# A hybrid Fourier and state-space layer on one core: the product of C with the entering states changes sides

## The chip, the core and the metric

The kernel runs on one core of one Trainium2 chip. The metric is the device time of one execution in microseconds (us), the median over the runs shown. The profiled execution is a further one, and its time stands beside its span below.

## The reference, cut to what matters

One layer works on 1152 tokens (128 of context, 1024 of latents) with 1024 features. After a normalisation and one wide product, one branch takes a Fourier transform, the other a bidirectional state-space scan (SSD) in chunks of 128 tokens; both are gated, merged and projected. The part that the change touches is the last line but one of the scan: the states that enter a chunk are read by that chunk's C, and each token and head is scaled by exp(acs), the decay since the chunk's start (in either direction).

```
acs = cumsum(dt * a) within the chunk
y_diag = einsum("bclgn,bcsgn,bgrcls,bcsgrp->bclgrp", cc, bc, lmat, xdt)
y_off  = einsum("bclgn,bcgrpn,bgrcl->bclgrp", cc, states_in, exp(acs))
y = y_diag + y_off
```

There are 8 groups (g) of 4 heads with 64 features each, states of 128, 9 chunks (c), and two directions (d). Chunk 0 is the context, for which no entering state is read.

## The kernel before, in words

**Engines and names.** PE is TensorE, DVE VectorE, ACT ScalarE, POOL GpSimd, SP the engine whose queue issues nearly all loads and stores. All data is float32. Large products run as three matmuls in the type float32r on split operands (high and low part, helper mm3, lines 99 to 103; the split itself is a ScalarE cast and a VectorE subtraction, lines 87 to 90); small products run as plain float32 matmuls, which the trace shows as two instructions each. The order of TensorE's instructions is the program's; the order on the other engines is laid out when the program is built, by when their inputs are expected (line 66 takes TensorE alone out of that).

**The SSD stage.** For each group g (lines 643 to 680) TensorE computes the columns of the wide product for B (tile bt), two chunks of x (xs), C (ct), some gate columns and z, each as a GEMM of 3 tiles x 8 x 3 matmuls of 384 columns. The small work of the scan is sewn into these GEMMs by a clock: `tick()` advances after every six such matmuls, and `at(step, t1, t2, ...)` resumes a Python generator at those ticks. So a GEMM has 12 ticks, and three ticks are 18 large matmuls plus what is sewn in between.

**The steps.** `tr_b` and `tr_x` (lines 514 to 534) transpose B and x to token-major (bn, xb). `states` (542 to 566) builds the entering states st[k] of both directions one after the other: weighted x (xw), split (xhl, in the e buffers), products (PSUM tile st), and a VectorE multiplication by decB and an addition. `outputs` (568 to 609) runs once per group and chunk, in the order 0, 4, 5, 3, 6, 2, 7, 1, 8, one chunk every three ticks, each in three sub-steps three ticks apart:
- first: load ab (acs of the chunk, broadcast to all partitions, 512 KB, two buffers) and, for c > 0, ea (exp(acs), two loads of 128 KB, three buffers); GpSimd masks ab into e (two selects, lines 582 and 583; three e buffers), eight ScalarE exponentials, one VectorE addition e+e;
- second: the product of B and C (cb, line 590), and VectorE multiplies it into e;
- third: for c > 0 the product po of the entering states with C, the states being the stationary side (line 597): four float32 matmuls with the result in the layout features by tokens; VectorE multiplies it by ea (599), GpSimd adds the two directions (600); four float32 matmuls y of x with e (605); VectorE adds y, then ea, to xs (607, 609).

Sub-steps of neighbouring chunks share a tick: third of one, second of the next, first of the one after.

**Around it.** dt_phase (348 to 435) computes the decays once, feature-major, and stores acs to d_acs and exp(acs) to d_eac, from where ab and ea are loaded; dt_natural (437 to 446) transposes two of its results to token-major (kwN). After a group's outputs, `gated` multiplies by z, `norm` normalises (616 to 641), and the next group's second GEMM writes xs again. All small products draw their PSUM tiles from five shared buffers (gps, line 121). After the last group four gate GEMMs cover the loads of the Fourier branch (685 on), which reuses the memory.

Of the kernel before, what the change touches and what calls it, by code (L numbers as in the profile page):

```python
# [12 lines left out]
F32 = mybir.dt.float32  # L13
F32R = mybir.dt.float32r
# [48 lines left out]
def tile_step(ctx, tc, a, o):  # L63
# [61 lines left out]
    d_acs = dp.tile([NCH, 64, P], F32, name="d_acs")  # L125
    d_eac = dp.tile([NCH, 64, P], F32, name="d_eac")
    d_dec = dp.tile([64, 8], F32, name="d_dec")
# [11 lines left out]
    make_identity(nc, ident)  # L139
    ones = cp.tile([P, P], F32, name="ones")  # L140
    V.memset(ones, 1.0)
    onesr = cp.tile([P, P], F32R, name="onesr")
    V.tensor_copy(onesr, ones)
    eps1 = cp.tile([P, 1], F32, name="eps1")
# [90 lines left out]
    sc = cp.tile([P, KT, 32], F32, name="sc")  # L235
    with pool("sp") as sp:
        xt = []
        for k in range(KT):
# [108 lines left out]

    def dt_phase(buf, w, kwN, decB):
        dtc = cp.tile([P, 3], F32, name="dtc")
# [3 lines left out]
        act(dtc[:, 2:3], dtc[:, 1:2], AF.Exp)  # L353
        xall, eall = buf[:, 0 : 5 * P], buf[:, 5 * P : 10 * P]
        G.memset(xall[64:P, 4 * P :], 0.0)
# [19 lines left out]
        def part(k0, k1):  # L375
# [27 lines left out]
            for h0 in (0, 64):  # L403
# [6 lines left out]
                V.tensor_copy(tot[bw, k0:k1].unsqueeze(2), sv[bw, :, 0:1])  # L410
            act(y_, s_, AF.Exp)
            for h0, c0, c1 in ((0, k0, k1), (64, 5 + k0, min(5 + k1, NCH))):
                for dst, src in ((d_acs, s_), (d_eac, y_)):
                    nc.sync.dma_start(dst[c0:c1].rearrange("c q l -> q c l"),
                                      src.rearrange("p (c l) -> p c l", l=P)[h0 : h0 + 64, 0 : c1 - c0])
            tt(x_, x_, s_, ALU.subtract)
# [17 lines left out]
        at(part(2, 5), DTT[1])  # L434
        at(dt_natural(xall, eall, kwN), DTT[2])

    def dt_natural(xall, eall, kwN):
        for k0, k1 in ((0, 2), (2, 5)):
            for w, src in enumerate((xall, eall)):
                ps = gps(f"dtt{k0}{w}")  # L440
                for k in range(k0, k1):
                    PE.transpose(ps[:, (k - k0) * P : (k - k0 + 1) * P], src[:, k * P : (k + 1) * P], ident)
                pv = ps[:, 0 : (k1 - k0) * P].rearrange("p (c h q) -> p h c q", h=2, q=64)
                for h, c0, c1 in ((0, k0, k1), (1, 5 + k0, min(5 + k1, NCH))):
                    V.tensor_copy(kwN[:, c0:c1, w * 64 : w * 64 + 64], pv[:, h, 0 : c1 - c0])
        yield
# [28 lines left out]
    with pool("sd") as sd, pool("ss") as ss, pool("sx", side="right") as sx:  # L475
# [3 lines left out]
        kwv = kwN.rearrange("p c (w d g h) -> p c w d g h", w=2, d=2, g=NG)  # L479
        knv, wsv = kwv[:, :, 0], kwv[:, :, 1]  # L480

        cr = [ss.tile([P, PADW + 1], F32, name=f"cr{i}") for i in range(2)]
        for t_ in cr:
# [3 lines left out]
        dt_phase(ss.tile([P, NCH, 256], F32, tag="xb", name="dtx").rearrange("p c q -> p (c q)"),  # L487
                 ss.tile([P, 8, P], F32R, tag="ct", name="w_dt"), kwN, decB)
        gate(3)
# [52 lines left out]
        def states(g, k, xb, bn, sts):  # L542

            cf, cb = (0, 0) if k < 0 else (1 + k, 8 - k)
            xw = ss.tile([P, 2, 256], F32, tag="xw", name=f"xw{g}_{k}", bufs=1)
            xhl = ss.tile([P, 2, 2, 256], F32R, tag="e", name=f"xhl{g}_{k}", bufs=3)
            xh, xl = xhl[:, 0], xhl[:, 1]
            for d, c in ((0, cf), (1, cb)):
                tt(xw[:, d].rearrange("p (j h q) -> p j h q", j=2, h=2), xb[:, c].rearrange("p (j h q) -> p j h q", j=2, h=2),
                   wsv[:, c, d, g, :].rearrange("p (h j) -> p j h", h=2).unsqueeze(3).broadcast_to([P, 2, 2, 64]), ALU.mult)  # L550
            split(xh, xl, xw)
            yield
            ps = gps(f"st{g}_{k}")
            if k < 0:
                mm3(ps, (bn[:, 0, 0], bn[:, 1, 0]), [x.rearrange("p d q -> p (d q)") for x in (xh, xl)], True, True)
                so = ss.tile([P, 1024], F32, tag="ab", name=f"so{g}", bufs=2)[:, 0:512]
                S.copy(so, ps)
                nc.sync.dma_start(o["sout"][g], so)
                return
            st = sts[0]  # L560
            for d, c in ((0, cf), (1, cb)):
                mm3(ps[:, d * 256 : d * 256 + 256], (bn[:, 0, c], bn[:, 1, c]), (xh[:, d], xl[:, d]), True, True)
            tt(st[:, k + 1].rearrange("p d (h q) -> p d h q", h=4), st[:, k].rearrange("p d (h q) -> p d h q", h=4),
               decv[:, :, g, :, k].unsqueeze(3).broadcast_to([P, 2, 4, 64]), ALU.mult)
            sv = st[:, k + 1].rearrange("p d q -> p (d q)")
            tt(sv, sv, ps, ALU.add)

        def outputs(g, c, bt, ct, xs, xb, st):
# [4 lines left out]
                              d_acs[c].rearrange("(d g q) l -> g d (q l)", d=2, g=NG)[g].partition_broadcast(P))  # L573
            if c > 0:

                ea = ss.tile([P, 2, 2, P], F32, tag="ea", name=f"ea{g}_{c}", bufs=3)
                for r0 in range(2):
                    nc.sync.dma_start(ea[r0 * 64 : r0 * 64 + 64].rearrange("p d j l -> p d (j l)"),
                                      d_eac[c].rearrange("(d g h j) l -> g h d (j l)", d=2, g=NG, h=2)[g, r0].partition_broadcast(64))
            e = ss.tile([P, 2, 4, P], F32, tag="e", name=f"e{g}_{c}", bufs=3)  # L580
# [9 lines left out]
            PE.matmul(pcb[:, 0:P], bt[:, cc], ct[:, cc], start=True, stop=True)  # L590
            tt(e[:, 0], e[:, 0], pcb[:, 0:P].unsqueeze(1).broadcast_to([P, 4, P]), ALU.mult)
            yield
            if c > 0:
                po = gps(f"po{g}_{c}")
                for d, k in ((0, c - 1), (1, 8 - c)):
                    for j in range(2):
                        PE.matmul(po[:, (2 * d + j) * P : (2 * d + j + 1) * P], st[:, k, d, j * P : j * P + P],  # L597
                                  ct[:, cc], start=True, stop=True)
                tt(ea, po.rearrange("p (d j l) -> p d j l", d=2, j=2), ea, ALU.mult)
                G.tensor_tensor(ea[:, 0], ea[:, 0], ea[:, 1], op=ALU.add)  # L600
            py = gps(f"y{g}_{c}")
            for j in range(2):
                for h in (2 * j, 2 * j + 1):
                    r0 = (h % 2) * 64
                    PE.matmul(py[r0 : r0 + 64, j * P : j * P + P], xb[:, c, h * 64 : h * 64 + 64], e[:, 0, h % 2 * 2 + j],  # L605
                              start=True, stop=True, tile_position=(0, r0))
            tt(xs[:, :, cc], xs[:, :, cc], py[:, 0 : 2 * P].rearrange("p (j l) -> p j l", j=2), ALU.add)
            if c > 0:
                tt(xs[:, :, cc], xs[:, :, cc], ea[:, 0], ALU.add)

# [32 lines left out]
        for g in range(NG):  # L643
# [21 lines left out]
            for i, c in enumerate((0, 4, 5, 3, 6, 2, 7, 1, 8)):  # L665
                t = 20 + 3 * i
                at(outputs(g, c, bt, ct, xs, xb, st), t - 6, t - 3, t)
            done = clock[0] + t
            gate(GATES[g])
# [479 lines left out]
```

## Time and profile before

| what | value |
|---|---|
| median of 3 runs | 1737.99 us (1735.97 to 1738.11) |
| profiled execution, its own time | 1733.38 us |
| its span, first to last instruction | 1731.6 us |
| granted TensorE clock over the span | 0.996 of full speed |
| SSD stage, groups 0 to 7 | about 115 to 1102 us of the span |

The profile covers one execution. "Busy" is the time in which an engine has an instruction under way; TensorE's are pipelined and overlap, so their durations add up to more than the time they take, and start-to-start distances are the better measure. "PEld" is the loading of stationary operands. A line such as "A <-B 4.4, 5" under the waits means that A stood idle until B was done, 4.4 us in 5 waits.

### The profile page before, as it was taken

The numbers are of one execution on the slowest core, as the hardware profiler recorded it, in microseconds if no ns is written. First come the engines' busy times: TensorE is split into PE (matmuls) and PEld (weight loads), VectorE is DVE, ScalarE is ACT, GpSimd is POOL, SyncE is SP. The second block draws the span as 40 slices with busy tenths as digits, with TensorE's granted clock in tenths as the row PEclk, the third lists the DMA queues.
The fourth block names the chain that finished last, engine by engine and source line by source line (L and its number), as shares of the span: only waits on it lengthen the run. The fifth ranks groups of instructions, "written<-read, shape, count | busy, mean of one in ns | idle before, by whom it ended". The sixth has DMA issues, their size and how long they took to land.

```text
span 1731.6 us, 27916 instructions
## 1 busy us (share of the span) xinstructions
PE 1706.1 (99%) x10728; PEld 1641.4 (95%) x10728; DVE 1093.1 (63%) x1876; ACT 809.8 (47%) x1666; POOL 184.7 (11%) x266
## 2 busy tenths in 40 slices
PE   7999999999999999999999999999999999999998
PEld 5999999999999999999999999999988999999987
DVE  6665877866857757757757758687487324444432
ACT  5445665565566576566466565415333211112221
POOL 1200210300300300301301202402000000000000
PEclk9999999999999999999999999999999999999999
DMA  9242633523524624524523525461066646643432
GB/s 349 80 102 59 152 103 104 142 92 99 149 76 114 140 70 118 141 77 114 135 75 106 140 77 146 148 228 54 16 214 217 229 146 229 220 168 120 161 122 73
DMA packets 110136, 229.63 MB, mean 133 GB/s; under 512 B 20594, under 2 KB 56436, under 8 KB 108340
## 3 DMA queue, kind: packets, MB, share of 16 engines
q1 hardware_dynamic: 108708, 223.14, 42.7%
q0 software_dynamic: 1296, 4.72, 0.7%
q8 instruction: 84, 1.38, 0.3%
q14 instruction: 48, 0.39, 0.1%
HBM read 187.24 MB, written 40.58 MB: 132 GB/s over the span
## 4 chain that ended last, share of the span: by engine, by line
PE 93%; DMA 3%; DVE 2%; issue 1%; ACT 0%; POOL 0%; SPq 0%; DVEq 0%; POOLq 0%; ACTq 0%
PE mm_g L101 5%; PE mm_g L103 5%; PE mm_g L102 5%; PE mm_x L101 4%; PE mm_x L103 4%; PE mm_x L102 4%; PE mm_z L101 3%; PE mm_z L103 3%; PE mm_z L102 3%; PE po L597 2%; PE y L605 2%; PE mm_b L101 2%; PE mm_c L101 2%; PE mm_b L103 2%; PE mm_c L103 2%; PE mm_b L102 2%
## 5 line engine op out<-in xcount | busy, mean ns | idle before, releaser
L73 ACT ACTIVATE e<-e,kwN 128x128 f32<-128x128 f32 x576 | 179.3, 390 | 110.9 <-POOL e L582 108.6
L101 PE MATMUL mm_g<-hT,wh_g 128*128 128x384 f32 x528 | 182.1, 345 | 0.0
L103 PE MATMUL mm_g<-hT,wl_g 128*128 128x384 f32 x528 | 177.9, 337 | 0.0
L102 PE MATMUL mm_g<-hT,wh_g 128*128 128x384 f32 x528 | 177.5, 336 | 0.0
L582 POOL TENSOR_SCALAR_AFFINE_SELECT e<-ab 128x512 f32<-128x512 f32 x72 | 51.0, 709 | 790.0 <-PE st L103 659.2
L101 PE MATMUL mm_z<-hT,wh_z 128*128 128x384 f32 x384 | 133.9, 349 | 0.0
L101 PE MATMUL mm_x<-hT,wh_x 128*128 128x384 f32 x384 | 131.5, 342 | 0.0
L103 PE MATMUL mm_z<-hT,wl_z 128*128 128x384 f32 x384 | 129.4, 337 | 0.0
L103 PE MATMUL mm_x<-hT,wl_x 128*128 128x384 f32 x384 | 129.2, 337 | 0.0
L102 PE MATMUL mm_x<-hT,wh_x 128*128 128x384 f32 x384 | 129.0, 336 | 0.0
L102 PE MATMUL mm_z<-hT,wh_z 128*128 128x384 f32 x384 | 129.0, 336 | 0.0
L101 PEld LDWEIGHTS mm_g<-hT,wh_g 128*128 128x128 f32 x528 | 99.3, 188 | 0.5 <-issue 0.2
L102 PEld LDWEIGHTS mm_g<-hT,wh_g 128*128 128x128 f32 x528 | 99.4, 188 | 0.4
L103 PEld LDWEIGHTS mm_g<-hT,wl_g 128*128 128x128 f32 x528 | 99.1, 188 | 0.0
L101 PEld LDWEIGHTS mm_z<-hT,wh_z 128*128 128x128 f32 x384 | 72.3, 188 | 0.9 <-issue 0.9
L101 PEld LDWEIGHTS mm_x<-hT,wh_x 128*128 128x128 f32 x384 | 72.1, 188 | 0.3
L102 PEld LDWEIGHTS mm_z<-hT,wh_z 128*128 128x128 f32 x384 | 72.3, 188 | 0.0
L102 PEld LDWEIGHTS mm_x<-hT,wh_x 128*128 128x128 f32 x384 | 72.3, 188 | 0.0
L103 PEld LDWEIGHTS mm_z<-hT,wl_z 128*128 128x128 f32 x384 | 72.1, 188 | 0.0
L103 PEld LDWEIGHTS mm_x<-hT,wl_x 128*128 128x128 f32 x384 | 72.1, 188 | 0.0
L597 PE MATMUL po<-ct,st 128*128 128x128 f32 x512 | 67.4, 274 | 0.0
L597 PEld LDWEIGHTS po<-ct,st 128*128 128x128 f32 x512 | 66.2, 191 | 0.0
(420 smaller groups left out, 4734.7 us busy)
## 6 DMA issues: line engine op xcount, KB each, us to landing
ab<-d_acs SPq DMA_DIRECT2D x72, 512.0 KB, 5.6
ea<-d_eac SPq DMA_DIRECT2D x128, 128.0 KB, 3.6
wr_g<-in_w_in SPq DMA_DIRECT2D x24, 512.0 KB, 5.5
yr<-d_y SPq DMA_DIRECT2D x16, 576.0 KB
aw<-in_ada_ss SPq DMA_DIRECT2D x8, 1024.0 KB, 5.2
wr_x<-in_w_in SPq DMA_DIRECT2D x16, 512.0 KB, 4.2
wr_z<-in_w_in SPq DMA_DIRECT2D x16, 512.0 KB, 3.6
d_y<-xs SPq DMA_DIRECT2D x16, 512.0 KB, 2.6
```

The lines of the kernel that those rows point to most:

```text
L73: S.activation(out, in_, func, bias=bias, scale=scale, **kw)
L101: PE.matmul(ps, lhs[0], rhs[0], start=first, stop=False)
L102: PE.matmul(ps, lhs[0], rhs[1], start=False, stop=False)
L103: PE.matmul(ps, lhs[1], rhs[0], start=False, stop=last)
L582: G.affine_select(e[:, 0], ab[:, 0], [[0, 4], [1, P]], ALU.is_ge, -1e30, base=0, channel_multiplier=-1)
L597: PE.matmul(po[:, (2 * d + j) * P : (2 * d + j + 1) * P], st[:, k, d, j * P : j * P + P], ct[:, cc], start=True, stop=True)
L605: PE.matmul(py[r0 : r0 + 64, j * P : j * P + P], xb[:, c, h * 64 : h * 64 + 64], e[:, 0, h % 2 * 2 + j], start=True, stop=True, tile_posit ...
```

## The change

The sides of po are exchanged. C (ct of the chunk, 128 columns) becomes the stationary side, the states of both directions (512 columns) the moving side, both split into high and low parts, so that po is three float32r matmuls of 512 columns with tokens on the partitions. The split is made in the second sub-step into a new tile sh with one buffer: two ScalarE casts and two VectorE subtractions, of 128 and of 512 columns. The two states needed are read by one strided view. The decay exp(acs) is then wanted by tokens: dt_natural transposes one more result into the new tile evN, once, and VectorE multiplies po by it as a broadcast. So the loads ea, and d_eac with its stores, go. GpSimd's addition of the directions stays. Its result is by tokens, so a new fourth sub-step, three ticks later, transposes it back with two matmuls, and VectorE adds that from PSUM to xs. The end of a group's outputs (done) moves by three ticks. The tile ea is now [128, 2, 256] with two buffers, which xw shares (xw had one of its own). The tile ones moves into a pool that is freed early.

```diff
-    d_eac = dp.tile([NCH, 64, P], F32, name="d_eac")
...
-    ones = cp.tile([P, P], F32, name="ones")
-    V.memset(ones, 1.0)
     onesr = cp.tile([P, P], F32R, name="onesr")
-    V.tensor_copy(onesr, ones)
...
     with pool("sp") as sp:
+        ones = sp.tile([P, P], F32, name="ones")
+        V.memset(ones, 1.0)
+        V.tensor_copy(onesr, ones)
...
-            act(y_, s_, AF.Exp)
+            act(yall[:, sl], s_, AF.Exp)
             for h0, c0, c1 in ((0, k0, k1), (64, 5 + k0, min(5 + k1, NCH))):
-                for dst, src in ((d_acs, s_), (d_eac, y_)):
-                    nc.sync.dma_start(dst[c0:c1].rearrange("c q l -> q c l"),
-                                      src.rearrange("p (c l) -> p c l", l=P)[h0 : h0 + 64, 0 : c1 - c0])
+                nc.sync.dma_start(d_acs[c0:c1].rearrange("c q l -> q c l"),
+                                  s_.rearrange("p (c l) -> p c l", l=P)[h0 : h0 + 64, 0 : c1 - c0])
...
-            for w, src in enumerate((xall, eall)):
+            for w, src in enumerate(alls):
                 ps = gps(f"dtt{k0}{w}")
...
-                    V.tensor_copy(kwN[:, c0:c1, w * 64 : w * 64 + 64], pv[:, h, 0 : c1 - c0])
+                    if w < 2:
+                        V.tensor_copy(kwN[:, c0:c1, w * 64 : w * 64 + 64], pv[:, h, 0 : c1 - c0])
+                        continue
+
+                    for c in range(c0, c1):
+                        S.copy(evN[:, c].rearrange("p (g j h) -> p g j h", j=2, h=2),
+                               pv[:, h, c - c0].rearrange("p (g h j) -> p g j h", h=2, j=2))
...
+        evN = sd.tile([P, NCH, 64], F32, name="evN")
+        evv = evN.rearrange("p c (d g h) -> p c d g h", d=2, g=NG)
...
-            xw = ss.tile([P, 2, 256], F32, tag="xw", name=f"xw{g}_{k}", bufs=1)
+            xw = ss.tile([P, 2, 256], F32, tag="ea", name=f"xw{g}_{k}", bufs=2)
...
-            if c > 0:
-
-                ea = ss.tile([P, 2, 2, P], F32, tag="ea", name=f"ea{g}_{c}", bufs=3)
-                for r0 in range(2):
-                    nc.sync.dma_start(ea[r0 * 64 : r0 * 64 + 64].rearrange("p d j l -> p d (j l)"),
-                                      d_eac[c].rearrange("(d g h j) l -> g h d (j l)", d=2, g=NG, h=2)[g, r0].partition_broadcast(64))
...
+            if c > 0:
+
+                sh = ss.tile([P, 2, 640], F32R, tag="sh", name=f"sh{g}_{c}")
+                b0, b1 = 2 * c - 2, 17 - 2 * c
+                q = 1 if b1 > b0 else -1
+                sv = st.rearrange("p k d q -> p (k d) q")[:, b0 : b1 + q : b1 - b0]
+                split(sh[:, 0, 512:], sh[:, 1, 512:], ct[:, cc])
+                split(*(sh[:, i, 0:512].rearrange("p (d q) -> p d q", d=2) for i in range(2)), sv)
             yield
             if c > 0:
+
                 po = gps(f"po{g}_{c}")
-                for d, k in ((0, c - 1), (1, 8 - c)):
-                    for j in range(2):
-                        PE.matmul(po[:, (2 * d + j) * P : (2 * d + j + 1) * P], st[:, k, d, j * P : j * P + P],
-                                  ct[:, cc], start=True, stop=True)
-                tt(ea, po.rearrange("p (d j l) -> p d j l", d=2, j=2), ea, ALU.mult)
+                mm3(po, (sh[:, 0, 512:], sh[:, 1, 512:]), (sh[:, 0, 0:512], sh[:, 1, 0:512]), True, True)
+                ea = ss.tile([P, 2, 256], F32, tag="ea", name=f"ea{g}_{c}", bufs=2)
+                tt(ea.rearrange("p d (h q) -> p d h q", h=4), po.rearrange("p (d h q) -> p d h q", d=2, h=4),
+                   evv[:, c, :, g].unsqueeze(3).broadcast_to([P, 2, 4, 64]), ALU.mult)
                 G.tensor_tensor(ea[:, 0], ea[:, 0], ea[:, 1], op=ALU.add)
...
             tt(xs[:, :, cc], xs[:, :, cc], py[:, 0 : 2 * P].rearrange("p (j l) -> p j l", j=2), ALU.add)
+            yield
             if c > 0:
-                tt(xs[:, :, cc], xs[:, :, cc], ea[:, 0], ALU.add)
+                pt = gps(f"yt{g}_{c}")
+                for j in range(2):
+                    PE.transpose(pt[:, j * P : j * P + P], ea[:, 0, j * P : j * P + P], ident)
+                tt(xs[:, :, cc], xs[:, :, cc], pt[:, 0 : 2 * P].rearrange("p (j l) -> p j l", j=2), ALU.add)
...
-                at(outputs(g, c, bt, ct, xs, xb, st), t - 6, t - 3, t)
-            done = clock[0] + t
+                at(outputs(g, c, bt, ct, xs, xb, st), t - 6, t - 3, t, t + 3)
+            done = clock[0] + t + 3
```

## Rows read from the trace of the kernel before

**Rows 1.** The page: busy time of each engine, and the chain that ended last.
```profile
PE 1706.1 (99%) x10728; PEld 1641.4 (95%) x10728; DVE 1093.1 (63%) x1876; ACT 809.8 (47%) x1666; POOL 184.7 (11%) x266
...
PE 93%; DMA 3%; DVE 2%; issue 1%; ACT 0%; POOL 0%; SPq 0%; DVEq 0%; POOLq 0%; ACTq 0%
```
**Rows 2.** Waits of TensorE and of SP's queue: us, times, longest us.
```profile
PE y L605 <- DVE e L79: 4.4, 5, 1.7
...
SPq L578 <- DVE xs L79: 84.0, 31, 6.0
```
**Rows 3.** Two stretches of the fifth group: length, each engine's busy time, clock, DMA.
```profile
686.40:703.60 17.20, 17.20 (x127) 16.35 (x126) 15.52 (x26) 11.79 (x34) 6.32 (x9) 1.00 0.62 164
703.60:728.80 25.20, 25.20 (x181) 23.72 (x180) 17.35 (x33) 12.47 (x37) 8.88 (x13) 1.00 0.62 142
```
**Rows 4.** TensorE's timeline, one output step: start us, us, engine, line.
```profile
601.33 1.05 PE L597 MATMUL po<-ct,st 128*128 128x128 f32 x8
602.31 0.66 PE L605 MATMUL y<-e,xb 128*64 128x128 f32 x8
```
**Rows 5.** TensorE's timeline: a context state's three matmuls of 512 columns, and the next.
```profile
667.83 0.39 PE L101 MATMUL st_-1_6764<-xhl_-1_6718,bn 128*128 128x512 f32 x1
...
668.52 0.34 PE L101 MATMUL mm_g<-hT,wh_g 128*128 128x384 f32 x1
```
**Rows 6.** TensorE's timeline: two transposes between matmuls of 384 columns.
```profile
664.46 0.38 PE L531 MATMUL tr<-ident,xs 128*128 128x128 f32 x2
664.59 0.43 PE L101 MATMUL mm_g<-hT,wh_g 128*128 128x384 f32 x1
664.86 0.34 PE L102 MATMUL mm_g<-hT,wh_g 128*128 128x384 f32 x1
```
**Rows 7.** Groups by line: busy us, mean ns, idle before and its releaser.
```profile
L531 PE MATMUL tr<-ident,xs 128*128 128x128 f32 x144 | 22.2, 272 | 0.0
...
L79 DVE TENSOR_TENSOR xs<-xs,ea 128x256 f32<-128x256 f32 x64 | 36.4, 569 | 23.2 <-POOL ea L600 23.1
...
L79 DVE TENSOR_TENSOR xs<-xs,y 128x256 f32<-128x256 f32 x72 | 29.7, 413 | 5.5 <-PE y L605 5.5
```
**Rows 8.** Timelines of ScalarE and VectorE: splits of 128 and of 512 columns.
```profile
259.78 0.27 ACT L521 CAST bn<-tb 128x128 fp32r<-128x128 f32 x1 [0.58 <-PE tb L519]
...
671.21 0.61 ACT L89 CAST xhl<-xw 128x512 fp32r<-128x512 f32 x1
...
260.08 0.29 DVE L79 TENSOR_TENSOR bn<-tb,bn 128x128 fp32r<-128x128 f32 x1 [0.16 <-ACT bn L521]
...
664.54 0.69 DVE L79 TENSOR_TENSOR xhl_-1_6718<-xw_-1_6717,xhl_-1_6718 128x512 fp32r<-128x512 f32 x1
```
**Rows 9.** The chain that ended last, around one late y of the fourth group.
```profile
572.62 8.27 DMA ab<-d_acs
...
586.46 0.61 DVE e L79
...
587.20 0.66 PE y L605 x8
```
**Rows 10.** The page's DMA issues: count, KB each, median us to landing.
```profile
ab<-d_acs SPq DMA_DIRECT2D x72, 512.0 KB, 5.6
```
**Rows 11.** Timelines in the overlap, third chunk with states: e on VectorE, y on TensorE.
```profile
699.95 0.68 DVE L79 TENSOR_TENSOR e<-e,cb 128x512 f32<-128x512 f32 x1
...
703.63 0.66 PE L605 MATMUL y<-e,xb 128*64 128x128 f32 x8
```
**Rows 12.** Timelines after the first group: last convolution step, first transposes of x.
```profile
273.37 1.36 DVE L76 SCALAR_TENSOR_TENSOR xs<-cr,xs 128x1154 f32<-128x1154 f32 x1 [1.39 <-ACT cr L73]
...
277.38 0.60 PE L531 MATMUL tr<-ident,xs 128*128 128x128 f32 x4
```
**Rows 13.** Timelines after the last group: a late Fourier fold, its first use.
```profile
1163.76 1.22 DVE L739 TENSOR_TENSOR xf<-xf,xf 126x1024 f32<-126x1024 f32 x1
...
1171.00 0.39 PE L777 MATMUL ta<-csg,xf 128*128 128x130 f32 x2
```

More of the change, by code (lines that the diff above doesn't have):

```diff
@@ L345, in tile_step, with dt_phase @@
         V.tensor_copy(rcol, ps[:, 0:10])
-    def dt_phase(buf, w, kwN, decB):
+    def dt_phase(buf, w, kwN, evN, decB):
         dtc = cp.tile([P, 3], F32, name="dtc")
@@ L353, in dt_phase @@
         act(dtc[:, 2:3], dtc[:, 1:2], AF.Exp)
-        xall, eall = buf[:, 0 : 5 * P], buf[:, 5 * P : 10 * P]
+        xall, eall, yall = (buf[:, i * P : (i + 5) * P] for i in (0, 5, 10))
         G.memset(xall[64:P, 4 * P :], 0.0)
@@ L434, in dt_phase, with dt_natural @@
         at(part(2, 5), DTT[1])
-        at(dt_natural(xall, eall, kwN), DTT[2])
-    def dt_natural(xall, eall, kwN):
+        at(dt_natural((xall, eall, yall), kwN, evN), DTT[2])
+    def dt_natural(alls, kwN, evN):
         for k0, k1 in ((0, 2), (2, 5)):
-            for w, src in enumerate((xall, eall)):
+            for w, src in enumerate(alls):
                 ps = gps(f"dtt{k0}{w}")
@@ L487, in tile_step @@
         dt_phase(ss.tile([P, NCH, 256], F32, tag="xb", name="dtx").rearrange("p c q -> p (c q)"),
-                 ss.tile([P, 8, P], F32R, tag="ct", name="w_dt"), kwN, decB)
+                 ss.tile([P, 8, P], F32R, tag="ct", name="w_dt"), kwN, evN, decB)
         gate(3)
```

## The prediction, made before the changed kernel had run

> **What bounds the kernel now.** I read the page first: the share of each engine and the chain that ended last [rows 1]. TensorE is busy for 99% of the span and holds 93% of the chain, so time is won by giving TensorE less to do or less to wait for, and lost wherever it waits longer. Then I read TensorE's timeline, where start-to-start distances tell what an instruction takes of a pipelined engine; durations overlap. Then the waits, to find where TensorE stands still in the SSD stage: almost nowhere, 4.4 us in 5 waits, all of the y matmuls for VectorE's e [rows 2]. Last, two stretches of one group, to see how much room VectorE and ScalarE have for what the change gives them [rows 3].
>
> **A. TensorE's product.** Before, an output step with c > 0 has 8 po instructions (4 matmuls in plain float32, each two instructions); from the first po to the first y it is 602.31 - 601.33 = 0.98 us [rows 4]. They go. In their place come three split-float matmuls of 512 columns and two 128x128 float32 transposes. The trace has both shapes. Three such matmuls with 512 columns in a row take 668.52 - 667.83 = 0.69 us [rows 5]. Two transposes between matmuls of 384 columns: from the first transpose to the second regular matmul is 664.86 - 664.46 = 0.40 us, less the 0.175 us of the regular one (17 of them lie between 664.86 and 667.83, [rows 5, 6]), so 0.225 us; this contains the slow restart after a float32 instruction. Sum 0.915 us, 0.065 us less, over 8 groups x 8 chunks = 64 steps: **-4.2 us**. Bounds: if the longer 512-column matmul hides the restart, two transposes cost only the 0.13 us from 664.46 to 664.59, and A is 64 x -0.16 = -10.2 us; if each transpose took its whole mean duration of 272 ns [rows 7], the step would be 1.23 us and A would be +16.3 us. I take the nearest rows, which have the shapes themselves.
>
> **B. The decays by tokens.** Five more transposes once, at 0.225 / 2 each: **+0.6 us** on TensorE. Nine ScalarE copies of 64 columns, at most 0.27 us each by a copy of twice the size [rows 8], come once where ScalarE has room; nothing. The constant tile that moves into another pool keeps its instructions; nothing.
>
> **C. The loads that go.** 128 loads of ea leave SP's queue, with 4 stores of d_eac. SP stood at these loads' line for 84.0 us behind VectorE's xs additions alone [rows 2], and the loads of ab, the gate stores and the weight loads queue behind it. From ab the line runs on: GpSimd's two selects, eight exponentials, e+e on VectorE, and in VectorE's order behind that ea and e times cb, and then y on TensorE. In the fourth group the ab load took 8.27 us, against a median of 5.6 us, and y came behind it [rows 9, 10]. Bounds: the five waits stay (0) or go (-4.4). I take **-4.4 us**, since each such chain begins with a load in that queue, which loses these 128 requests and no longer stands still for VectorE's additions. What is late next if it isn't SP: the select's e buffers, three shared with xhl, which the change leaves alone.
>
> **D. The split and its new wait.** For each of the 64 steps ScalarE gets two casts, 0.27 us (128 columns) and 0.61 us (512), and VectorE two subtractions, 0.29 and 0.69 us [rows 8]: 0.98 us of VectorE, 63 us in all. These are off TensorE's path as long as VectorE has room, and the cover goes if it hasn't: po now waits for them, one step (three ticks) after they are issued, and there is one sh buffer, so ScalarE's casts also wait for the po before, with its later exponentials behind them. Where the state updates are over, five steps in 25.2 us hold 17.35 us of VectorE [rows 3]: 4.9 more fits. ScalarE's 12.47 + 5 x 0.88 fits too. Where they overlap, three steps in 17.20 us hold 15.52 us of VectorE, and with 2.94 it is 18.46: 1.3 us too much. The margin there: e times cb ends at 699.95 + 0.68 and y starts at 703.63, 3.0 us [rows 11]; po starts 0.98 earlier and the subtractions take 0.98 longer, so 1.0 us is left. Overrun less margin is 0.3 us a group, 8 groups: **+2.4 us**. Bounds 0 and the slower rival's price below. The product of ea stays one VectorE instruction of 512 columns; the last addition reads PSUM instead of SBUF, which by the xs,y row takes 413 instead of 569 ns [rows 7]; I leave that 0.16 us as reserve. GpSimd's add stays; its reader is now a transpose three ticks later, with 5 us for 0.7 us of work. xw and ea now share two buffers, but the xw steps end when the second ea begins; nothing. One more PSUM buffer of the five is used per step, so each comes round after about one step, 5 us, which is longer than the evacuations take.
>
> The Trainium skill (SBUF — State Buffer, section Who interferes with whom) says that a VectorE instruction with two SBUF inputs and a GpSimd one that reads SBUF exclude each other for a whole instruction. The two rows of xs additions fit that (569 ns with two SBUF inputs, 413 with one). By the rule each new subtraction pair can lose what that addition loses, 0.156 us, 0.47 us in three steps, D would be 8 x 0.77 = 6.2 us and the time 1736.7 us.
>
> **E. The fourth step.** The last addition to xs comes three ticks later, so in the groups where the outputs end after z, the normalisation shifts by 3 x 6 x 0.175 = 3.15 us. At the first group's end the next convolution is done at 273.37 + 1.36 = 274.73 and the transposes that need it start at 277.38: 2.65 us of room [rows 12], so 0.5 us late at worst, twice: I take **+0.5 us** of 0 to 1. At the last group the Fourier folds end near 1164.98 and TensorE uses them at 1171.00 [rows 13]: 6 us, covered.
>
> **Sum:** -4.2 + 0.6 - 4.4 + 2.4 + 0.5 = -5.1 us. The profiled execution took 1733.38 us (span 1731.6 and 1.8 around it), so it would take 1728.3. The median shown is 1737.99, 4.6 us above that execution; the same difference from it gives **1732.9 us**. A measurement of this kernel can tell about 0.2%, 3.5 us, from no change; this is 0.3%. With C and D at half and double of what I took, the forecast's own range is 1730 to 1736.
>
> **Rivals.**
> *Slower: the subtractions arrive behind a late e.* VectorE works in order, and the casts and subtractions are issued after e times cb. If the ab load still comes late once a group, po waits where y waited, plus the subtractions and the product. In the fourth group e times cb begins at 586.46 and takes 0.61; with 0.98 for the subtractions and 0.69 for po, y starts at 588.7 instead of 587.20: 1.5 us [rows 9]. In all 8 groups 12 us; with A, B and E +8.9: **1746.9 us**. It decides from the point where e times cb ends less than 1.65 us before y would start. For: five of the y already start as soon as they can. Against: in the overlapped steps the margin is 3.0 us. Chance 0.27.
> *No change: the load of ab stays last.* Its 5.6 us [rows 10] are longer than a step of 5 us; if the five waits stay (C = 0) the sum is -0.7: **1737.3 us**. For: the chain of rows 9 starts with ab, not with ea. Against: SP's standing time. Chance 0.22.
> *A larger gain:* the restart hides under 512 columns and VectorE is never late: -10.2 + 0.6 - 4.4 = -14.0: **1724.0 us**. Chance 0.10.
> *Transposes that take their duration:* +16.3 for A, 1753.4 us. Against it stand rows 6: two in 0.225 us. Chance 0.03. The Trainium skill (TensorE: Matmul & The Clock Gate, Part 4: PE-mode transpose) gives about 275 ns for one in a kernel; the trace's 272 ns agrees as a duration, and the spacing in rows 6 speaks against its use as a cost.
>
> **How the numbers follow.** My forecast has 0.38, with the larger gain 0.48 for faster by over 0.2%; no change 0.22; slower 0.27 + 0.03 = 0.30. The range reaches from the larger gain, 1724, to the slower rival with a microsecond for a second late step, 1748, and leaves out the transposes' case and the tails.
>
> **What would show it.** A: three po matmuls 0.23 us apart, two transposes in 0.13 and a slow next matmul. C: no wait of y for e, ab under its 5.6 us. D: waits of po for sh; none or tenths of a microsecond in steps 2 to 4 of each group if I am right; over 1 us and in the later steps if the slower rival is. E: the first tr of the second and last groups. If TensorE's waits in the SSD stage add up to more than 10 us, the prediction is wrong in D; if po with its transposes takes 1 us or more, in A.

## The result and the profile after: 0.66% slower

| | before | after |
|---|---|---|
| median | 1738.05 us (4 runs) | 1749.51 us (4 runs, 1747.91 to 1752.01) |
| ratio, 95% interval | | 1.0066 (1.005 to 1.0082) |
| span of the profiled execution | 1731.6 us | 1747.6 us |

The forecast was 1732.9 us, faster. The page of the changed kernel, to be read against [rows 1]: VectorE has 59 us more, ScalarE 51 us more, and TensorE's busy time has not fallen.

```profile
PE 1711.7 (98%) x10541; PEld 1623.4 (93%) x10541; DVE 1152.0 (66%) x2004; ACT 861.1 (49%) x1805; POOL 192.1 (11%) x266
```

The waits of TensorE (us in total, times, longest us), to be read against [rows 2]. The y waits for e are gone, and two new waits stand there, of dtt and of yt; ps_s, between them, waits before as after (9.0 us, then 8.8).

```profile
PE dtt L440 <- DVE kwN L444: 10.7, 1, 10.7
PE ps_s L265 <- DVE sq L79: 8.8, 1, 8.8
PE yt L620 <- POOL ea L608: 3.8, 3, 2.8
```

**The first new wait** is one stall of 10.7 us, once in the execution. VectorE's timeline there (start us, us, engine, line, operation, in brackets the idle time before it and what ended it):

```profile
111.20 1.23 DVE L79 TENSOR_TENSOR wl_x<-wr_x,wh_x 128x1024 fp32r<-128x1024 f32 x1 [1.67 <-ACT wh_x L89]
123.25 0.69 DVE L79 TENSOR_TENSOR st<-st,decB 128x512 f32<-128x512 f32 x1 [10.82 <-DMA decB<-d_dec]
123.96 1.81 DVE L444 COPY kwN<-dtt 128x128 f32<-128x128 f32 x8
```

VectorE waits for the load of decB, and the eight kwN copies, which need nothing of it, stand behind that wait. In the kernel before it was the same, as its timeline shows (TensorE, then VectorE), and nobody waited for the copies:

```profile
115.75 1.25 PE L442 MATMUL dtt<-ident,dtx 128*128 128x128 f32 x10
127.71 0.69 DVE L79 TENSOR_TENSOR st<-st,decB 128x512 f32<-128x512 f32 x1 [11.95 <-DMA decB<-d_dec]
128.42 1.81 DVE L445 COPY kwN<-dtt 128x128 f32<-128x128 f32 x8
```

Its ten transposes fill four PSUM tiles of the pool's five. The change adds a third source, so fifteen transposes fill six; the sixth tile has to wait until a kwN copy has emptied one. TensorE takes its instructions in order, so the whole GEMM waits with it. Behind the stall the matmuls of 384 columns start 0.32 us apart instead of 0.175. The windows (from:to, length, busy time of PE, PEld, DVE, ACT, POOL, granted clock, DMA share, GB/s) show the clock at half, 1.2 GHz (0.50), then full again, 2.4 GHz (1.00):

```profile
113.00:125.20 12.20, 1.54 (x13) 1.33 (x11) 1.93 (x7) 0.76 (x5) 0.00 (x0) 0.74 0.50 80
125.20:129.00 3.80, 3.80 (x14) 3.80 (x13) 0.56 (x3) 0.68 (x5) 0.00 (x0) 0.50 0.00 0
129.00:133.00 4.00, 4.00 (x24) 4.00 (x24) 0.00 (x0) 0.48 (x1) 0.00 (x0) 1.00 0.00 0
```

Twelve matmuls took 125.12 to 129.06, 3.94 us instead of 12 x 0.175 = 2.1: 1.8 us more. The stall and its echo are 12.5 us, of the 16 us by which the spans differ. Most of the rest is the second wait: the fourth group, counted from its first matmul of B to the next group's, takes 132.5 us instead of 127.6.

**The second new wait** is of yt, the transposes back, for GpSimd's addition of the directions. The timeline around the longest one, in the fourth group: GpSimd, and TensorE's first instruction after the wait:

```profile
585.22 1.08 POOL L583 TENSOR_SCALAR_AFFINE_SELECT e<-ab 128x512 f32<-128x512 f32 x1
590.35 0.71 POOL L582 TENSOR_SCALAR_AFFINE_SELECT e<-ab 128x512 f32<-128x512 f32 x1 [4.05 <-DMA ab<-d_acs]
591.01 1.08 POOL L583 TENSOR_SCALAR_AFFINE_SELECT e<-ab 128x512 f32<-128x512 f32 x1
592.07 1.69 POOL L608 TENSOR_TENSOR ea<-ea 128x256 f32<-128x256 f32 x1
...
593.81 0.69 PE L620 MATMUL yt<-ident,ea 128*128 128x128 f32 x2 [2.82 <-POOL ea L608]
```

The same picture: an instruction that needs nothing of a load stands on its engine behind one that waits for it. Here too the clock was at half afterwards:

```profile
593.80:600.10 6.30, 6.29 (x24) 5.21 (x25) 4.60 (x8) 3.31 (x11) 2.02 (x3) 0.50 0.71 151
```

**The step itself**, TensorE's timeline in the fifth group, against [rows 4]. From yt to y it is 713.52 - 712.51 = 1.01 us, where po took 0.98 before:

```profile
712.51 0.38 PE L620 MATMUL yt<-ident,ea 128*128 128x128 f32 x2
712.65 0.48 PE L101 MATMUL po<-sh 128*128 128x512 f32 x1
712.96 0.40 PE L102 MATMUL po<-sh 128*128 128x512 f32 x1
713.19 0.40 PE L103 MATMUL po<-sh 128*128 128x512 f32 x1
713.52 0.55 PE L613 MATMUL y<-e,xb 128*64 128x128 f32 x6
```

**VectorE's room.** The stretches that answer to [rows 3], from the y of the same chunks on:

```profile
702.30:719.70 17.40, 17.40 (x123) 15.58 (x122) 15.95 (x25) 14.38 (x42) 8.35 (x10) 1.00 0.67 166
719.70:745.20 25.50, 25.42 (x165) 21.88 (x163) 22.82 (x46) 15.53 (x45) 7.34 (x11) 1.00 0.39 79
```

VectorE holds 22.82 us of 25.5 in the second one: what step D said (17.35 + 4.9), and nearly full.

### The profile page after: what moved, and what is told of

The parts are those of the page before. It is cut to its first block, busy times and chain, and to the rows that moved or that the text cites. A ratio compares the mean times of both kernels' runs of the same rounds, so it can differ in the third digit from the quotient of the medians.

```text
span 1747.6 us, 27582 instructions
## 1 busy us (share of the span) xinstructions
PE 1711.7 (98%) x10541; PEld 1623.4 (93%) x10541; DVE 1152.0 (66%) x2004; ACT 861.1 (49%) x1805; POOL 192.1 (11%) x266
## 5 line engine op out<-in xcount | busy, mean ns | idle before, releaser
L101 PE MATMUL mm_b<-hT,wh_b 128*128 128x384 f32 x192 | 66.3, 345 | 0.0
L101 PE MATMUL mm_c<-hT,wh_c 128*128 128x384 f32 x192 | 65.4, 341 | 0.0
```

The lines of the kernel that those rows point to most:

```text
L101: PE.matmul(ps, lhs[0], rhs[0], start=first, stop=False)
```

## The experiments

Every ratio is against the kernel before on the same chip, with a 95% interval. Line numbers differ by a few between kernels.

### Is it the one stall? Mend it, and put it into the kernel before

**The third source later.** The changed kernel, with the third source at another tick:

```diff
-        at(dt_natural((xall, eall, yall), kwN, evN), DTT[2])
+        at(dt_natural(((0, xall), (1, eall)), kwN, evN), DTT[2])
+        at(dt_natural(((2, yall),), kwN, evN), DTT[2] + 14)
```

> The changed kernel, with the transposes and copies of the third source (the decays by tokens) 14 ticks after the other two, so that no stage takes more than five PSUM tiles at once. Theory 1 (one stall): TensorE's 10.7 us wait at the dtt transposes for a VectorE kwN copy, and the half clock right behind it (12 matmuls at 0.32 instead of 0.175 us, 1.8 us), make the loss. Then the wait is gone, the first group takes about 12.5 us less, and the time is 1749.5 - 12.5 = 1737.0 us. Theory 2 (the cost lies in the 64 steps): the step costs 64 x more than before and the wait only overlaps it; then the time stays over 1745 us. Theory 3 (the wait moves): what stood behind VectorE's in-order queue is late next, and a wait of 5 us or more stands elsewhere in the first group; 1742 us or more.

**The third source in the kernel before.** Its dt_natural gets the same third source, with the tiles and copies that belong to it; the result (evN) is not read. One line of the edit:

```diff
-        at(dt_natural(xall, eall, kwN), DTT[2])
+        at(dt_natural((xall, eall, yall), kwN, evN), DTT[2])
```

> The kernel before, with the third source of the decays by tokens added at the same tick (five transposes, nine ScalarE copies, two more PSUM tiles) and its result not used; all else, the ea loads too, as before. Theory 1 (one stall): six PSUM tiles for a pool of five make TensorE wait for a VectorE copy there, and the clock falls behind it: before + 11 to 13 us, 1749 to 1751 us, with a wait of dtt for kwN of 10 to 11 us. Theory 2 (the cost lies in the 64 steps): only five transposes are added, before + 0.6 us, 1738.7 us.

**The copies on ScalarE.** The changed kernel with six tiles at one tick, and another engine to empty them:

```diff
-                        V.tensor_copy(kwN[:, c0:c1, w * 64 : w * 64 + 64], pv[:, h, 0 : c1 - c0])
+                        S.copy(kwN[:, c0:c1, w * 64 : w * 64 + 64], pv[:, h, 0 : c1 - c0])
```

> The changed kernel, with all six PSUM tiles of the decays at the same tick as there, and the kwN copies on ScalarE instead of VectorE. Theory 1 (the copies stand on VectorE behind an instruction that waits for the decB load; the sixth tile alone would cost nothing if its releaser were free): the 10.7 us wait goes or falls below 3 us, and the time is that of e1_yall_later, a ratio of 1.004 to 1.006. Rival (six tiles for five buffers cost it whatever engine copies): a wait of 8 us or more stays and the ratio is that of the changed kernel or above.

*Measured.* The kernel before with the third source: 1.0094 (1.0074 to 1.0114), and the same wait appears, alone:

```profile
PE dtt L442 <- DVE kwN L446: 12.1, 1, 12.1
```

Its first group, from the first matmul of B to that of the next group's B, grew by 15.9 us (109.1 to 124.9); the rest of the span shrank by 2. With the third source later that part is 109.0 us (121.9 in the changed kernel); with the copies on ScalarE it is 109.0 too, and dtt waits for nothing in either. So six tiles cost no wait where the engine that empties them is free; the cause is the queue that the copies stand in. **That this makes the wait is shown in both directions.** But the whole time fell less than the 12.5 us expected: 1.0055 (1.0042 to 1.0069) with the third source later, 1.0049 (1.0032 to 1.0066) with the copies on ScalarE. Other losses stood up in its place. With the third source later the profiled execution has a wait for wl_g that the changed kernel's hasn't, and its longest wait of yt is in another group:

```profile
PE yt L621 <- POOL ea L609: 4.5, 4, 2.9
PE mm_g L103 <- DVE wl_g L79: 2.7, 1, 2.7
```

### The end of the last group: the load of ex

The timeline of that kernel (the third source later) ahead of the wl_g wait: VectorE, and SyncE's queue (SPq) with the last store of xs and the load of ex:

```profile
1129.99 1.21 DVE L79 TENSOR_TENSOR wl_g<-wr_g,wh_g 128x1024 fp32r<-128x1024 f32 x1
...
1130.46 0.45 SPq L654 DMA_DIRECT2D d_y<-xs  x1
...
1131.93 0.59 SPq L727 DMA_DIRECT2D ex<-d_ex  x1
...
1144.21 1.53 DVE L79 TENSOR_TENSOR ex<-ex 32x256 f32<-32x256 f32 x4 [13.01 <-DMA ex<-d_ex]
...
1147.65 1.22 DVE L79 TENSOR_TENSOR wl_g<-wr_g,wh_g 128x1024 fp32r<-128x1024 f32 x1
```

In the kernel before, ex was issued at 1118.91, between the stores of the last xs, and VectorE did not wait for it. In the changed kernel and its mended versions it stands behind all four stores, and so behind VectorE's last work on xs; the next weight split is queued on VectorE behind ex. The fourth step alone does not do this: in the kernel before with only that step (further below) ex is issued at 1119.24, between the stores, and VectorE does not wait for it. Which part of the change moves the load was not tried. The edit gives the load another queue, in the kernel with the third source later and in the changed kernel as it is:

```diff
-        nc.sync.dma_start(ex, d_ex.rearrange("n o (c j) -> (o c) n j", j=P))
+        nc.scalar.dma_start(ex, d_ex.rearrange("n o (c j) -> (o c) n j", j=P))
```

> As e1_yall_later, and the load of ex at the start of the Fourier stage is issued by ScalarE instead of SyncE, where it stood behind the four stores of the last group's xs. Theory 1 (the fourth step makes this load late): VectorE stood 13.0 us for ex with a weight split behind it, TensorE 2.7 us for that split and 1.7 us at half clock after it; these go: 3 to 5 us below e1_yall_later, a ratio to before of about 1.003 in place of 1.0055. Rival (the weights of that gate are late anyway, through the DMA engines): the wait for wl_g stays, ratio 1.005 to 1.006.

> The changed kernel as it is, with the load of ex issued by ScalarE. In its own profiled execution VectorE stood 7.6 us for ex, yet TensorE did not wait for the weight split behind it. Theory 1 (the order of SyncE's queue costs the changed kernel itself in most executions): 3 to 7 us below the changed kernel, a ratio to before of 1.002 to 1.005. Theory 2 (it costs only the mended versions, whose last group ends at another point of the weights' loads): the ratio stays at 1.006 to 1.007.

*Measured.* Mended so: 1.0014 (1.0002 to 1.0026), where the third source later alone gave 1.0055; 7 us by the ratios (3 to 5 were expected), and no wait for wl_g. On the changed kernel as it is, nothing was won: 1.01 (1.0078 to 1.0121), above what either theory allowed. So this load costs the mended version and not the changed kernel, where VectorE stood 7.6 us for ex and TensorE did not wait for the split behind it. Why the load comes later in the mended version (12.3 us from its issue to VectorE's start, 7.8 in the changed kernel) was not tried. The profiled execution of the changed kernel with this load on ScalarE shows five waits of yt for GpSimd, 7.2 us, where the changed kernel's had three, 3.8 us; that they make it slower is not shown.

The four ratios read together give the price of the stall. With ex on ScalarE, moving the third source takes the kernel from 1.01 to 1.0014, 15 us, close to the 16 us that the stall costs alone in the kernel before (1.0094). With ex on SyncE the same move gives 2 us. 7 of the 13 us between are the late weight split, which then takes the stall's place; the other 6, by which the changed kernel is slower with ex on ScalarE, stay unexplained.

### GpSimd's addition

Three edits on the kernel with the third source later: the addition on VectorE (the first diff line pair), GpSimd's instructions in the order of the program text, so that an addition stands ahead of the selects (the second pair), and, with ex on the other queue as well, the transposes back two ticks later (the third).

```diff
-                G.tensor_tensor(ea[:, 0], ea[:, 0], ea[:, 1], op=ALU.add)
+                tt(ea[:, 0], ea[:, 0], ea[:, 1], ALU.add)
...
-    ctx.enter_context(tc.manual_schedule(engines={mybir.EngineType.PE}))
+    ctx.enter_context(tc.manual_schedule(engines={mybir.EngineType.PE, mybir.EngineType.Pool}))
...
-                at(outputs(g, c, bt, ct, xs, xb, st), t - 6, t - 3, t, t + 3)
+                at(outputs(g, c, bt, ct, xs, xb, st), t - 6, t - 3, t, t + (5 if i < 8 else 3))
```

> As e1_yall_later, and the addition of the two directions of ea on VectorE instead of GpSimd. Theory 1 (GpSimd's in-order queue): the addition stands behind a select that waits for the ab load; the three waits of the transposes back for it (3.8 us) and the half clock behind the one in the fourth group (2 us or so) go: 4 to 6 us below e1_yall_later. Rival (VectorE is full): 64 x 0.33 us more on VectorE and one more pair of SBUF inputs make e, the split or the evacuations late: the same as e1_yall_later or up to 6 us above it, with new waits for VectorE.

> As e1_yall_later, and GpSimd's instructions stand in the order of the program text: the addition of a chunk's two directions ahead of the two selects of the chunk after the next, where it stood behind them. Theory 1 (the addition stands behind a select that waits for its load): TensorE's waits of yt for GpSimd (4.5 us in 4 waits) go: 3 to 5 us below e1_yall_later, a ratio of about 1.003. Rival (the selects now stand behind an addition that waits for po): e comes later, y waits for e instead, ratio 1.0055 or more.

> As e5_ex_other_queue, and the transposes back of a chunk stand two ticks later (2.1 us), except those of a group's last chunk. Theory 1 (the addition on GpSimd is late by 2.8 us at most, once in a run, and half clock follows): nearly all of the wait of yt for GpSimd goes, with the slow matmuls behind it: 2 to 4 us below e5_ex_other_queue, a ratio to before of 0.999 to 1.000. Rival (what is late then is e, sh or a weight split, and the time only moves there): a ratio of 1.001 or more, with those waits in the trace.

*Measured.* All three took the waits of yt away, and none was faster: 1.0165 (1.0152 to 1.0179) on VectorE and 1.0072 (1.0052 to 1.0091) in program order, against 1.0055 for the same kernel without that; 1.0029 (1.0018 to 1.0041) two ticks later, against 1.0014. The waits moved to VectorE. The addition there made the weight splits late:

```profile
PE mm_z L103 <- DVE wl_z L79: 7.1, 3, 2.4
PE mm_g L103 <- DVE wl_g L79: 5.9, 2, 3.5
PE mm_b L103 <- DVE wl_b L79: 4.8, 2, 2.4
```

Two ticks later, po waited for the split:

```profile
PE po L102 <- DVE sh L79: 6.9, 8, 1.2
```

In program order po waited for sh as well (2.3 us in 9 waits), and 7.8 us were lost at the start of the Fourier stage (26.1 us from the first matmul of tile fw to that of eb, 18.3 before), where small float32 matmuls (tb, ta) waited 1.1 and 0.9 us for VectorE and the clock then stood at half; whether that belongs to the new order was not tried, and the kernel with the copies on ScalarE met the same. So Theory 1 fell each time. The rivals named the right engine and not always the size or the wait: on VectorE the addition cost 19 us where up to 6 were allowed, and in program order it was po that waited, not y. VectorE is nearly full, and what is taken off GpSimd's path came back as a wait for VectorE.

### TensorE's step: a change of type, or the hand-over to y?

The 1.01 us had two candidates. In one, each change between plain float32 and float32r costs 0.1 us; then placing the transposes of the chunk before between po and y, beside float32 work, saves one. The edit to the kernel with the third source later keeps the two transposes and their addition in a function, called one chunk on:

```diff
                 mm3(po, (sh[:, 0, 512:], sh[:, 1, 512:]), (sh[:, 0, 0:512], sh[:, 1, 0:512]), True, True)
+                if pend:
+                    pend.pop()()
...
+                pend.append(back)
             yield
+            if c == NCH - 1:
+                pend.pop()()
```

> As e1_yall_later, and the two transposes back of a chunk stand between the next chunk's po and y matmuls (plain float32 beside plain float32), so that TensorE changes between the two float types once less in a step. Theory 1 (the change of type costs about 0.1 us each time, in a step 1.01 us for po and transposes against 0.98 before): 64 x 0.1 = 6 us below e1_yall_later. Rival (the excess belongs to the first float32 instruction's weight load or to the PSUM bank, not to the change of type): within 2 us of e1_yall_later.

*Measured.* 1.0087 (1.0074 to 1.01), slower than the 1.0055 of the same kernel without it, with po waiting for sh (5.6 us in 9 waits). The step without waits, from the matmul before yt or po to the second one behind cb, has a median of 2.269 us, against 2.2815 in the kernel with the third source later and 2.250 before: 0.0125 us saved, not 0.1. My theory of the types fell. What is left is arithmetic on TensorE's start times: y starts 0.33 us behind the third po matmul (713.52 - 713.19), where matmuls of 512 columns are 0.23 apart, 0.10 more; before, it started 0.205 us behind the last of the 0.11 us po instructions, again 0.09 more. The hand-over to y costs a tenth in either kernel. My sum of 0.915 for the new side had left it out; the 0.98 of the old side held it.

### The other steps, alone in the kernel before

The splits, with nobody to read them (sh is a tile of one half, and the low part overwrites the high one):

```diff
             tt(e[:, 0], e[:, 0], pcb[:, 0:P].unsqueeze(1).broadcast_to([P, 4, P]), ALU.mult)
+            if c > 0:
+                sh = ss.tile([P, 640], F32R, tag="sh", name=f"sh{g}_{c}")
...
+                split(sh[:, 512:], sh[:, 512:], ct[:, cc])
+                sw = sh[:, 0:512].rearrange("p (d q) -> p d q", d=2)
+                split(sw, sw, sv)
```

> The kernel before, with the two casts (ScalarE) and two subtractions (VectorE) of each of the 64 steps added; nobody reads their result. Theory 1 (step D of the prediction: VectorE has the room, 0.3 us a group at most): before + 0 to 2.4 us. Theory 2 (VectorE's room is spent, weight splits, e and evacuations come late): before + 5 us or more, with waits of TensorE for wl tiles or e that the kernel before has not.

No ea loads (and no d_eac stores); the kernel leaves the decays of the entering states out, so it shows a cost and is no version to use:

```diff
-                for r0 in range(2):
-                    nc.sync.dma_start(ea[r0 * 64 : r0 * 64 + 64].rearrange("p d j l -> p d (j l)"),
...
-                tt(ea, po.rearrange("p (d j l) -> p d j l", d=2, j=2), ea, ALU.mult)
+                tt(ea.rearrange("p d j l -> p (d j) l"), po.rearrange("p (q l) -> p q l", q=4),
+                   ones.unsqueeze(1).broadcast_to([P, 4, P]), ALU.mult)
```

> The kernel before, without the 128 loads of ea and the 4 stores behind them; the product of po multiplies by ones, so the decays of the entering states are left out of the result. Theory 1 (step C of the prediction): the 4.4 us in which y waited for e go: before - 3 to -5 us. Rival (the load of ab is late by its own 5.6 us): the waits stay, before - 0 to -1 us.

The fourth step alone, and then without the ea loads as well (the decays left out again):

```diff
+            yield
             if c > 0:
                 tt(xs[:, :, cc], xs[:, :, cc], ea[:, 0], ALU.add)
...
-                at(outputs(g, c, bt, ct, xs, xb, st), t - 6, t - 3, t)
-            done = clock[0] + t
+                at(outputs(g, c, bt, ct, xs, xb, st), t - 6, t - 3, t, t + 3)
+            done = clock[0] + t + 3
```

> The kernel before, with only the fourth step: the last addition to xs three ticks later, and the gating and normalisation of each group behind it. Theory 1 (step E of the prediction, the shift itself is covered): before + 0 to 1 us. Theory 2 (the shift makes the end of the last group late and with it the start of the Fourier stage): before + 3 us or more, with a wait of TensorE between the last group and the Fourier stage.

> The kernel before without the ea loads (the decays of the entering states are left out of the result, as in e8_no_ea_loads) and with the fourth step. Theory 1 (steps C and E take away the same waits of y for e, 4.4 us, so their gains do not add): a ratio of 0.995 to 0.997, as e8_no_ea_loads alone. Theory 2 (separate causes): 0.996 x 0.997 = 0.993.

*Measured.*

| in the kernel before | ratio | in 1735 us |
|---|---|---|
| splits alone | 1.0008 (0.9996 to 1.002) | +1.4 |
| no ea loads | 0.9961 (0.9946 to 0.9977) | -6.8 |
| fourth step alone | 0.9972 (0.9961 to 0.9984) | -4.9 |
| no ea loads and fourth step | 0.9954 (0.9937 to 0.997) | -8.0 |

The waits of y for e, 4.4 us before, are all gone without the loads; the fourth step alone leaves these:

```profile
PE y L605 <- DVE e L79: 1.7, 2, 1.4
```

and the splits alone have more of them:

```profile
PE y L614 <- DVE e L79: 8.5, 8, 2.1
```

The fourth step was forecast to cost 0 to 1 us and gained 4.9, so neither theory held there. Its likely reason stands in [rows 7]: VectorE's addition of ea to xs stood 23.1 us for GpSimd's addition, with VectorE's later work behind it. Three ticks later it stands half as long:

```profile
L79 DVE TENSOR_TENSOR xs<-xs,ea 128x256 f32<-128x256 f32 x64 | 35.8, 559 | 11.3 <-POOL ea L600 11.3
```

It is the same picture as the two new waits, read from two profiles and not isolated by a run. So steps C and E take away largely the same waits, and their gains don't add. With the splits (+1.4), TensorE's step (+2.0, below) and five transposes (+0.6) the parts sum to -4.0 us, a ratio of 0.9977; the best mended version has 1.0014. I put the 6 us between down to what the parts do to each other on VectorE and GpSimd; the three edits to the addition point there, but none isolates it. Its profile agrees: the fourth group, with a wait of yt of 2.8 us for GpSimd and half clock behind it, takes 131.3 us, against 126.5 in the kernel without loads and with the fourth step, 4.8 more.

### Looking for a faster version

If the loads are the gain, ScalarE can work ea out of ab, which is there on all partitions, with no new split:

```diff
-                    nc.sync.dma_start(ea[r0 * 64 : r0 * 64 + 64].rearrange("p d j l -> p d (j l)"),
...
+                    act(ea[r0 * 64 : r0 * 64 + 64], ab[r0 * 64 : r0 * 64 + 64, :, 2 * r0 : 2 * r0 + 2], AF.Exp)
```

> The kernel before, with ea (the decays by tokens, on the partitions of each head) worked out by ScalarE from ab, two exponentials of 64 partitions and 512 elements a step, instead of loaded; d_eac goes. Theory 1 (what the change gains comes from the loads that go, and it can be had without a new split): VectorE and TensorE keep their work, ScalarE gets 64 x 1.2 us where it is busy for 47% of the span; before - 4 to -7 us, a ratio of 0.996 to 0.998. Rival (ScalarE's two exponentials stand ahead of the eight of e and make e late, or hold the ab buffer): the waits of y for e come back, a ratio of 1.000 or more.

> The kernel before with both the fourth step (as e12_fourth_step_alone) and ea worked out by ScalarE from ab (as e10_ea_from_ab). Theory 1 (both take away the same few late e): no better than the better of the two, a ratio of 0.996 to 0.998. Theory 2 (they add): e12's 0.997 and e10's 0.999 give 0.996 or less. Rival (the exponentials of ea fill ScalarE or hold ab in the overlapped steps): 0.999 or more, with waits of y for e.

*Measured.* Alone 0.999 (0.9977 to 1.0002), not to be told from before, and y still waits for e, 4.0 us in 8 waits; with the fourth step 1.0024 (1.0012 to 1.0036), slower, with 8.6 us of y waiting for e in 14 waits. The exponentials hold the ab buffer: in the first of the two, SyncE's load of ab waits for them, 72.0 us in 26 waits. So **the fastest version that computes the whole result is the kernel before with the fourth step alone, 0.9972**: one `yield` and three ticks.

## Why the prediction was wrong, step by step

**A, -4.2 us: mis-sized, it is +2.0.** This is worked out from steps without waits, as measured above, and no run isolates it. Per step +0.0315 us in 48 steps and +0.034 in each group's last, -0.2025 in the first of each group, which has no yt, and 0.225 for each group's lone last yt: 1.5 + 0.3 - 1.6 + 1.8 = +2.0. The rows were right (matmuls 0.23 us apart, two transposes with the slow restart behind them, which is the 0.31 us between the first two po matmuls); the sum compared a stretch that ends at y with one that doesn't. The prediction's own sign for A, 1 us or more, did show: 1.01.

**B, +0.6 us: the step that failed.** The price of the five transposes stands (no run isolates it), and "nothing" for the rest was wrong: the stall it left out is 12.5 us in the trace of the changed kernel, and 16 us by the ratio where it stands alone in the kernel before. "One more PSUM buffer of the five" was counted for the steps, under D, and never for dt_natural, where four tiles became six. The row that says it was in the trace of before: kwN copies 11 us behind the transposes, behind a wait for decB. I had asked what hides the copies on ScalarE and not who empties the tiles ahead of them.

**C, -4.4 us: right in its mechanism, -6.8 alone.** The waits went, and GpSimd's first select stands for the load of ab 12.9 us in 6 waits, where it was 61.2 in 24. It is not gone: the longest wait of yt goes back to one such load, for which GpSimd stood 4.05 us. What is late next in general stays open; SyncE's load of ab now stands for GpSimd's selects 150.5 us in 56 waits, 87.2 in 40 before.

**D, +2.4 us: in keeping with the splits (+1.4 alone, -0.7 to +3.5; po's weight loads waited 1.0 us in 3 waits for sh), wrong for "GpSimd's add ... 5 us for 0.7 us of work".** It looked at the addition's own length, not at the select ahead of it that waits for ab. The waits of yt are 3.8 us, and the group with the longest is 4.9 us longer. The Trainium skill (SBUF — State Buffer, section Who interferes with whom) has a GpSimd instruction that reads SBUF and a VectorE instruction with two SBUF inputs exclude each other. The trace agrees in the durations: the 512-column subtraction takes 908 ns on average in the changed kernel and 743 with the addition off GpSimd, against 0.69 in [rows 8]. By that rule D was to be 6.2 us; the splits alone measured 1.4, at most 3.5.

**E, +0.5 us: too small a question.** The shift alone is a gain (-4.9), and VectorE does not wait for ex there. The loss at the last group's end, in the versions without the stall, came through the order of SyncE's queue, which [rows 13], the Fourier folds, don't show.

**The rivals.** The slower one gave 1746.9 us, near the result, by a mechanism that was not there: the waits for sh are 1.0 us, not 12. Longer ones (2.3 to 6.9 us) appear only in versions in which yt waits no more. That the result is near its time is chance. The transposes cost what rows 6 said. The sign that laid more than 10 us of TensorE's waits to D pointed to the wrong letter: dtt's 10.7 us belong to B, ahead of the steps. And the forecast's own range of 1730 to 1736 does not follow from its rule: C and D at half and double, one at a time, give 1728.5 to 1735.3.

## What to carry to other kernels

Count PSUM tiles at every place that a change touches, one-time places too, and for each tile beyond the pool ask which engine empties it and what stands ahead of that copy in its queue; a late copy that costs nothing becomes a stall the moment somebody waits for it. When an engine's sum fits, ask next for the order: a short instruction behind one that waits for a load is as late as the load. And before a large change, try its smallest piece alone: here a `yield` held the gain.

## What the chip showed that I had not expected

A wait of TensorE can cost more than its own length, or not. After 10.7 and 2.8 us of waiting in the changed kernel the granted clock was 0.50 (1.2 GHz) for 3.8 and 6.3 us. After 2.91 us of waiting for the same instruction in the kernel with the third source later it stayed at 1.00 (2.4 GHz); its window from the end of that wait on:

```profile
965.50:971.50 6.00, 5.91 (x38) 5.11 (x38) 4.35 (x10) 4.78 (x16) 2.00 (x4) 1.00 0.57 175
```

And with the copies on ScalarE, waits of 0.9 and 1.1 us among the small float32 matmuls at the Fourier stage's start were followed by this stretch, in a part (fw to eb, as above) that became 7.8 us longer:

```profile
1190.00:1200.00 10.00, 9.77 (x38) 8.21 (x37) 6.96 (x37) 5.82 (x18) 0.00 (x0) 0.50 0.00 1
1200.00:1210.00 10.00, 10.00 (x67) 10.00 (x67) 6.35 (x30) 4.01 (x13) 0.00 (x0) 0.82 0.00 0
```

What decides it is not told apart by these runs. It may be one reason why the mended versions scatter (1737.88 to 1746.92 us with the third source later); that is not shown.
